# Down projection of an encoder block's FFN: ten blocks in five pairs, seven products a pair

## Chip, cores, metric

The kernel runs on one core of a Trainium2 chip. The metric is the device time of one execution in microseconds (us). The core has five engines with a queue each: PE (TensorE, matrix products into PSUM), DVE (VectorE), ACT (ScalarE), POOL (GpSimd) and SP (SyncE, which here only issues transfers). POOL issues transfers too, and only its transfers can add to what stands at their destination ("adding transfers", `accum_op=add`).

## What is computed

One layer of a hybrid encoder over 256 + 512 = 768 tokens of width 1024: three token mixers, gates, an output projection, and then the part that is changed, a SwiGLU FFN with residual:

```python
h2 = rmsnorm(x, ffn_norm_g[li])
g, up = jnp.split(h2 @ w_gate_up[li], 2, axis=-1)     # (768, 1024) @ (1024, 2 x 2816)
x = x + (jax.nn.silu(g) * up) @ w_down[li]            # (768, 2816) @ (2816, 1024)
```

All is float32.

## The kernel before

**Split numbers.** A float32 product is made of three passes: each operand is split into a high part hi (rounded to fp32r by an ACT copy) and a low part lo = x - hi (a DVE subtraction), and `mm3` (lines 756 to 758) issues hi·hi, hi·lo and lo·hi into the same PSUM tile. So every operand that PE reads costs an ACT and a DVE pass first.

**Weights.** `WStream` loads all weights in a fixed order (`W.add`), in halves of 128x1024 (512 KB, on SP's queue, three raw buffers), and `_split` makes hi and lo in rings of four tiles `wh`, `wl` each (lines 598 and 604). `W.get()` hands out the next weight and splits the one after it.

**FFN.** The 2816 hidden columns are 11 blocks of 256. For blocks 1 to 10 gate and up are products of 2x2 block matrices done with seven half-size products in place of eight (Strassen's scheme in Winograd's form): `right_factors` makes the factors of the normalized input F once, `_split_w` and `_factor` make those of each weight (five sums on POOL, lines 575 to 582; hi on ACT, line 560; lo on DVE, line 561), `block` runs the seven products of 12 matmuls of 384 columns and adds them up in two tiles `fs` (line 1412, DVE). `fin_gate` makes tanh of the gate on ACT and the gate's part of SiLU on DVE (line 1369) into `act_in` (tile `fa`); `fin_up` multiplies by up (line 1374; on POOL for blocks 1 to 10) and splits the result into the hidden activations `hid` (lines 1375, ACT, and 1376, DVE). Block 0 goes the plain way through `first`.

`down(fb)` is plain: for each of six tiles of 128 tokens and each half of the 1024 output columns, 2 x 3 matmuls of 512 columns into a PSUM tile `dn`, which DVE adds to the running output `x1` (line 1440). The order is gate 0, up 0, down 0, gate 1, up 1, and then for each further block gate `fb`, down `fb - 1`, up `fb`; the last down stores the output rows.

**PSUM.** In this stage there are eight banks: five of kind d, three of kind b. `down` takes one of each by turns, gate and up take d.

**Order of the work.** The program is written as one sequence; a planner with a timeline of its own then orders each engine's queue, by the place in the program and by what it estimates to be ready. `tc.keep_in_program_order` holds an instruction at its place. At run time every queue runs strictly in that order.

Of the kernel before, what the change touches and what calls it, by code (L numbers as in the profile page):

```python
# [504 lines left out]
class WStream:  # L505
# [2 lines left out]

    HALF = 1024

    def __init__(self, nc, tc, ctx):
# [18 lines left out]

    def _dma(self):
        i, h = divmod(self.n_dma, 2)
        ap, kk, cols, _ = self.src[i]
        t = self.praw.tile([128, self.HALF], F32, name=f"wr{i}_{h}", tag="wr")
        k2 = kk // 2
        tv = t.rearrange("p (k c) -> p k c", k=k2)
        n = cols // len(ap)
# [24 lines left out]
    def _split_w(self, i, h):  # L564
# [18 lines left out]
        self._factor(i, "S4", s4)  # L583
        self._factor(i, "A22", A22)

    def _split(self):
        i, h = divmod(self.n_split, 2)
        self.n_split += 1
        kind = self.src[i][3]
        if kind == "w":  # L590
# [7 lines left out]
        self.nc.scalar.activation(hi, r, AF.Copy)  # L598
        if self.by_dma:

            self.nc.scalar.activation(lo, r, AF.Copy, scale=-1.0)  # L601
            self.nc.gpsimd.dma_start(lo, r.bitcast(F32R), accum_op=ALU.add)  # L602
            return
        self.sub.tensor_tensor(out=lo, in0=r, in1=hi.bitcast(F32), op=ALU.subtract)  # L604
# [11 lines left out]
    def get(self, ahead=True):  # L616
        i = self.next
        self.next += 1
        if ahead:
            self.ahead(i + 1)  # L620
        _, kk, cols, kind = self.src[i]
        p = self.parts.pop(i)
        if kind == "w":
            return p
        k2 = kk // 2
        at = lambda t, k, c0, n: t[:, cols * (k % k2) + c0 : cols * (k % k2) + c0 + n]
        return lambda k, c0, n: tuple(at(t, k, c0, n) for t in p[k // k2])


def hybrid_block(ctx, tc, A, outs, consts):  # L630
# [45 lines left out]
    ones = cp.tile([128, 1], F32, name="ones")  # L676
    v.memset(ones, 1.0)
    subg = cp.tile([128, 1], F32, name="subg")


    warm = env.psa("warm")
# [41 lines left out]
    for what, fb in order:  # L723
        if what == "down":
            W.add(wd[:, 2 * fb : 2 * fb + 2, :], 2, 1024, "x")
        else:
            W.add(cols("w_gate_up", 256 * fb + (DFF if what == "up" else 0)), 8, 256, "w" if fb else None)


    def rsqrt(x, n, tag, bufs=4):  # L730

        i = sm.tile([128, n], I32, name=uid("rqi"), tag=f"rqi{n}")
        y = sm.tile([128, n], F32, name=uid("rqy"), tag=tag, bufs=bufs)
        t = sm.tile([128, n], F32, name=uid("rqt"), tag=f"rqt{n}")
# [97 lines left out]
    z_scr = [dr.tile([128, TOK], F32, name=f"z_scr{m}") for m in range(8)]  # L832
    gl_scr = [dr.tile([128, TOK], F32, name=f"gl_scr{m}") for m in range(24)]
    br_scr = [dr.tile([128, TOK], F32, name=f"br_scr{m}") for m in range(8)]
    mo_scr = [dr.tile([128, 8, TOK], F32, name=f"mo_scr{w}") for w in "hl"]


# [530 lines left out]
        act.activation(t[:, 0:n], c, AF.Tanh, scale=0.5)  # L1368
        v.scalar_tensor_tensor(out=act_in[fb][:, m, cs], in0=t[:, 0:n], scalar=1.0, in1=c, op0=add, op1=mul)

    def fin_up(fb, c, m, cs, eng=v):
        hh, hl = hid[fb]
        o = act_in[fb][:, m, cs]
        eng.tensor_tensor(out=o, in0=o, in1=c, op=mul)
        act.activation(hh[:, m, cs], o, AF.Copy, scale=0.5)
        v.scalar_tensor_tensor(out=hl[:, m, cs], in0=o, scalar=0.5, in1=hh[:, m, cs].bitcast(F32),
                               op0=mul, op1=sub)

    def new_block(what, fb):
        if what == "gate":  # L1380
            act_in[fb] = fa.tile([128, 2, TOK], F32, name=uid("fa"), tag="fa")
        else:
# [15 lines left out]
    def block(what, fb):  # L1398
# [18 lines left out]
        kw = {} if what == "gate" else {"eng": gp}  # L1417
        act.activation(c12, prod("A11", "B11"), AF.Copy)
        plus(c11, c12, prod("A12", "B21"))
        fin(fb, c11, 0, h1, **kw)  # L1420
# [5 lines left out]
        fin(fb, c22, 1, h2, **kw)  # L1426
        plus(c12, c12, prod("S4", "B22"))
        fin(fb, c12, 0, h2, **kw)
        plus(c21, c21, prod("A22", "T4"))
        fin(fb, c21, 1, h1, **kw)  # L1430

    def down(fb, last):
        w = W.get()
        x = hid.pop(fb)
        for tt in (3, 4, 5, 0, 1, 2) if fb else range(TILES):
            for c0 in (0, 512):
                ps = (psd if c0 else env.psb)("dn")
                dense_tm(ps, w, c0, 512, x, tt, 2)
                o = x1[tt][:, c0 : c0 + 512]
                v.tensor_tensor(out=o, in0=o, in1=ps, op=add)  # L1440
                if last:
                    nc.sync.dma_start(os_[tt][:, c0 : c0 + 512], o)


    with ExitStack() as c5:
# [92 lines left out]
        fa = c6.enter_context(tc.tile_pool(name="ffa", bufs=1))  # L1538
        ft_ = c6.enter_context(tc.tile_pool(name="fft", bufs=2))
        po, rs = [None] * TILES, [None] * TILES  # L1540

        def out_rows(w, c, kh, tt):
# [49 lines left out]
        rows(5)  # L1592


    W.extra = tuple(c6.enter_context(tc.tile_pool(name="wx" + w, bufs=1)) for w in "hl")
    W.sums = c6.enter_context(tc.tile_pool(name="wsum", bufs=3))
    tp = c6.enter_context(tc.tile_pool(name="ffT", bufs=1))
    fh = c6.enter_context(tc.tile_pool(name="ffh", bufs=1))
# [51 lines left out]
    down(0, False)  # L1650
    next(factors)
    next(factors, None)
    for what, fb in order[3:]:
        if what == "down":
            down(fb, fb == NFB - 1)
        else:
            block(what, fb)
    c6.close()
    x1ctx.close()

# [42 lines left out]
```

## Time and profile before

| | us |
|---|---|
| median of 3 runs | 1786.9 (1786.52 to 1790.95) |
| the profiled execution | 1785.8, of it 1784.0 span |
| PE, DVE, ACT, POOL busy | 1762.8, 1296.6, 871.6, 266.4 |
| FFN, from the first gate matmul to the end | 1266.7 to 1784.0 |
| one block of gate, down, up | about 45.5 |

A row of groups reads: line, engine, operation, output and input tiles, their shapes, count | busy time, mean ns of one | idle time of the engine just before them and what ended it. A row of waits: engine, tile and line that waited, what for: us in total, times, longest. A row of the order of time: start, duration, instruction, in brackets the idle time before it. A row of one tile or line: count: shortest, median, longest ns, first and last start. Durations of neighbours on an engine overlap a little, since an instruction starts before the one ahead has left the pipeline.

### The profile page before, as it was taken

The page shows a single profiled execution, that of the slowest core. Times are in us where ns is not written, and L with a number is a line of the kernel's source. Part 1 is how long each engine was busy: PE and PEld are TensorE (multiplying, and loading weights), DVE is VectorE, ACT ScalarE, POOL GpSimd, SP SyncE. Part 2 cuts the span into 40 slices and gives each one's busy share as a digit, 9 for nine tenths or more (in the row PEclk, how much of TensorE's full clock was granted, in tenths as well). Part 3 has the DMA queues.
Part 4 walks back from the last instruction along what each step waited for, and adds up shares of the span by engine and source line. Part 5 has one row for each costly group of instructions (what it writes and reads, how often), then busy time and mean ns, then how long its engine had stood idle before and what let it go on. Part 6 is the DMA issues. An engine that isn't in the chain of part 4 may idle for free.

```text
span 1784.0 us, 29452 instructions
## 1 busy us (share of the span) xinstructions
PE 1762.8 (99%) x11286; PEld 1625.7 (91%) x11286; DVE 1296.6 (73%) x2385; ACT 871.6 (49%) x1842; POOL 266.4 (15%) x280
## 2 busy tenths in 40 slices
PE   8999999999999999999999999999999999999998
PEld 8999988999999998999979888888889999999997
DVE  7655748799999579778875545442699777777775
ACT  7444544777676367778765433232333333333331
POOL 0000000000000101011110101000114333333330
PEclk9999999999999999999999999999999999999999
DMA  7222656655656477454862534331312222222221
GB/s 254 72 96 95 111 137 161 150 143 133 155 143 153 126 179 191 109 113 97 177 165 83 207 127 159 116 111 54 83 48 71 71 71 72 71 71 71 72 71 71
DMA packets 194797, 207.88 MB, mean 117 GB/s; under 512 B 57824, under 2 KB 167648, under 8 KB 194656
## 3 DMA queue, kind: packets, MB, share of 16 engines
q1 hardware_dynamic: 174656, 147.27, 27.9%
q0 software_dynamic: 18848, 55.58, 14.0%
q10 hardware_dynamic: 1152, 3.15, 0.5%
q8 instruction: 89, 1.46, 0.3%
q14 instruction: 52, 0.43, 0.1%
HBM read 146.11 MB, written 32.57 MB: 100 GB/s over the span
## 4 chain that ended last, share of the span: by engine, by line
PE 92%; DVE 3%; DMA 2%; ACT 1%; issue 1%; SPq 0%; POOL 0%; DVEq 0%; ACTq 0%; POOLq 0%
PE gl L756 4%; PE gl L757 4%; PE gl L758 4%; PE br L757 3%; PE br L756 3%; PE br L758 3%; PE dn L756 3%; PE dn L757 3%; PE dn L758 3%; PE gate L756 3%; PE gate L757 3%; PE gate L758 3%; PE up L756 3%; PE up L758 3%; PE up L757 3%; PE qk L756 2%
## 5 line engine op out<-in xcount | busy, mean ns | idle before, releaser
L598 ACT ACTIVATE wh<-wr 128x1024 fp32r<-128x1024 f32 x146 | 163.7, 1122 | 104.6 <-PE br L757 27.8
L604 DVE TENSOR_TENSOR wl<-wr,wh 128x1024 fp32r<-128x1024 f32 x100 | 130.7, 1307 | 92.1 <-ACT wh L598 91.3
L756 PE MATMUL gl<-Hhi,wh 128*128 128x256 f32 (+1 forms) x384 | 132.4, 345 | 1.1 <-ACT glt L1065 1.1
L1440 DVE TENSOR_TENSOR x<-x,dn 128x512 f32<-128x512 f32 x132 | 89.0, 685 | 57.5 <-PE dn L758 57.3
L758 PE MATMUL gl<-Hhi,wl 128*128 128x256 f32 (+1 forms) x384 | 129.0, 336 | 0.0
L757 PE MATMUL gl<-Hlo,wh 128*128 128x256 f32 (+1 forms) x384 | 128.9, 336 | 0.0
L602 POOL DMA_DIRECT2D wl<-wr x46 | 40.2, 873 | 518.0 <-ACT wl L601 486.3
L756 PE MATMUL qk<-wh,Hhi 128*128 128x256 f32 x384 | 108.4, 282 | 1.6 <-ACT qksq L1131 1.6
L757 PE MATMUL qk<-wl,Hhi 128*128 128x256 f32 x384 | 108.6, 283 | 0.0
L758 PE MATMUL qk<-wh,Hlo 128*128 128x256 f32 x384 | 108.5, 283 | 0.0
L560 ACT ACTIVATE wh_S<-ws 128x512 fp32r<-128x512 f32 x70 | 41.7, 623 | 130.8 <-PE dn L758 104.1
L756 PE MATMUL dn<-wh,hidh 128*128 128x512 f32 x264 | 102.5, 390 | 1.2 <-DVE x L1440 1.0
L757 PE MATMUL dn<-wl,hidh 128*128 128x512 f32 x264 | 103.0, 390 | 0.0
L758 PE MATMUL dn<-wh,hidl 128*128 128x512 f32 x264 | 100.9, 390 | 0.0
L756 PEld LDWEIGHTS gl<-Hhi,wh 128*128 128x128 f32 x384 | 72.3, 188 | 8.3 <-ACT glt L1065 1.3
L758 PEld LDWEIGHTS gl<-Hhi,wl 128*128 128x128 f32 x384 | 72.1, 188 | 8.0
L757 PEld LDWEIGHTS gl<-Hlo,wh 128*128 128x128 f32 x384 | 72.3, 188 | 7.1
L756 PEld LDWEIGHTS qk<-wh,Hhi 128*128 128x128 f32 x384 | 73.0, 190 | 2.5 <-ACT qksq L1131 1.8
L1231 DVE TENSOR_REDUCE nm<-sc 128x1 f32<-128x512 f32 (+1 forms) x96 | 57.1, 598 | 24.7 <-PE sc L1226 23.5
L758 PEld LDWEIGHTS qk<-wh,Hlo 128*128 128x128 f32 x384 | 73.1, 190 | 0.7
L757 PEld LDWEIGHTS qk<-wl,Hhi 128*128 128x128 f32 x384 | 73.1, 190 | 0.5
L1233 ACT ACTIVATE p<-sc,nm 128x512 f32<-128x512 f32 (+1 forms) x96 | 59.0, 616 | 12.4 <-DVE nm L1231 11.9
(455 smaller groups left out, 5944.9 us busy)
## 6 DMA issues: line engine op xcount, KB each, us to landing
wr<-in_w_in_dram SPq DMA_DIRECT2D x48, 512.0 KB, 5.5
wl<-wr POOLq DMA_DIRECT2D x46, 512.0 KB, 5.1
wr<-in_w_gate_up_dram SPq DMA_DIRECT2D x44, 512.0 KB, 3.5
wr<-in_w_branch_dram SPq DMA_DIRECT2D x24, 512.0 KB, 4.2
wr<-in_w_down_dram SPq DMA_DIRECT2D x22, 512.0 KB, 3.7
glr<-gl_scr POOLq DMA_DIRECT2D x24, 384.0 KB, 3.7
wr<-in_w_mem_kv_dram SPq DMA_DIRECT2D x16, 512.0 KB, 3.4
wr<-in_w_in_dram SPq DMA_DIRECT2D x32, 256.0 KB, 4.4
```

The costliest lines, as they stand in the source:

```text
L560: self.nc.scalar.activation(f(hi), src, AF.Copy)
L598: self.nc.scalar.activation(hi, r, AF.Copy)
L602: self.nc.gpsimd.dma_start(lo, r.bitcast(F32R), accum_op=ALU.add)
L604: self.sub.tensor_tensor(out=lo, in0=r, in1=hi.bitcast(F32), op=ALU.subtract)
L756: pe.matmul(ps, wh, xh, start=start, stop=False)
L757: pe.matmul(ps, wh, xl, start=False, stop=False)
L758: pe.matmul(ps, wl, xh, start=False, stop=stop)
L1231: v.tensor_reduce(out=nm[:, m : m + 1], in_=ps, axis=AX.X, op=ALU.max, negate=True)
L1233: act.activation(pm[:, 0:n], ps, AF.Exp, bias=nm[:, m : m + 1], accum_out=s1s[:, tt : tt + 1] if m == 0 else s2)
L1440: v.tensor_tensor(out=o, in0=o, in1=ps, op=add)
```

## The change

Blocks 1 to 10 are taken in pairs (1,2), (3,4), ... (9,10). The down projection of a pair is a 2x2 block product: A11, A21 are the two token halves of the first block's activations, A12, A22 those of the second; B11, B12 are the column halves of the first block's `w_down` rows, B21, B22 those of the second's. Seven products of half size (384 tokens x 256 x 512 columns, three PSUM tiles each) take the place of eight. The order becomes gate, up, gate, up, down of the pair.

The sums of the weights (T1 to T4) are made by adding transfers from DRAM (`_split_d`), those of the activations by DVE (`left_sum`); `left` and `_right` split them. Products that belong to one output quarter are added to `x1` by DVE at once (`into`). The three that belong to several quarters (P1, P6, P5) are copied out by ACT and added up over the pairs in DRAM tiles `p_scr` by adding transfers (`keep`); `down_sums` loads them in the last pair, between gate 9 and up 9, and DVE adds them to the quarters. Quarter (1,0) takes quarter (1,1) along, which is why (1,1) is subtracted from it once at block 2. The last pair does not go through `p_scr`: it adds P1 and P1 + P6 to `x1` by adding transfers in SBUF.

`hid` and its splits remain for block 0 only; `fin_up`'s multiplication goes from POOL to DVE; the ring of extra tiles for down weights goes; `act_in` has two buffers, the `ft` tiles (tanh, and now the copies of products) three.

```diff
 # WStream
+    def _right(self, i, key, src):
+        hi, lo = self._tile(f"{i}_{key}")
+        self.nc.scalar.activation(hi, src, AF.Copy)
+        self.nc.vector.tensor_tensor(out=lo, in0=src, in1=hi.bitcast(F32), op=ALU.subtract)
...
+    def _split_d(self, i, h, kind):
...
+        add = lambda t, b: self.nc.gpsimd.dma_start(t.rearrange("p (k c) -> p k c", k=2), b, accum_op=ALU.add)
+        minus = lambda t, x: self.nc.scalar.activation(t, x, AF.Copy, scale=-1.0)
+        new = lambda k: self.wsums.tile([128, self.HALF], F32, name=f"wt{i}{k}", tag="wt")
+        if kind == "d" and h == 0:
+            self._right(i, "B11", r)
+            self.z = new("z")
+            minus(self.z, r)
+            add(self.z, b12)
+        elif kind == "d":
+            self.x = new("x")
+            minus(self.x, r)
+            add(self.x, b22)
+            self._right(i, "T3", self.x)
+        elif h == 0:
+            add(self.x, b11)
+            self._right(i, "T2", self.x)
+            self._right(i, "T1", self.z)
+            self._right(i, "B21", r)
+        else:
+            minus(self.x, self.x)
+            add(self.x, b21)
+            self._right(i, "T4", self.x)
+            self._right(i, "B22", r)
 # order of the weights
-    order = [("gate", 0), ("up", 0), ("down", 0), ("gate", 1), ("up", 1)]
-    for fb in range(2, NFB):
-        order += [("gate", fb), ("down", fb - 1), ("up", fb)]
-    order.append(("down", NFB - 1))
...
+        elif fb % 2 == 0:
+            for b, kind in ((fb - 1, "d"), (fb, "e")):
+                W.add([wd[:, 2 * b : 2 * b + 2, 512 * c : 512 * c + 512] for c in range(2)], 4, 512, kind)
 # fin_up
-        eng.tensor_tensor(out=o, in0=o, in1=c, op=mul)
-        act.activation(hh[:, m, cs], o, AF.Copy, scale=0.5)
...
+        v.tensor_tensor(out=o, in0=o, in1=c, op=mul)
+        if fb == 0:
...
 # block
+        if what == "up" and fb % 2 == 0:
+            W.ahead(W.next + 1)
...
-    def down(fb, last):
...
+    def left(key, src):
+        hi, lo = (lf.tile([128, 2, HT], F32R, name=uid(f"l{key}{w}"), tag="l" + w) for w in "hl")
+        act.activation(hi, src, AF.Copy, scale=0.5)
+        v.scalar_tensor_tensor(out=lo, in0=src, scalar=0.5, in1=hi.bitcast(F32), op0=mul, op1=sub)
+        L[key] = hi, lo
...
+    def down_begin(fb):
+        a = act_in[fb]
+        left("A11", a[:, :, 0:HT])
+        left("S3", left_sum(None, a[:, :, 0:HT], a[:, :, HT:TOK], sub))
...
+    def into(r, c, y, op=add, done=False, pin=False):
+        for t in range(3):
+            o = out_block(r, c, t)
+            i = v.tensor_tensor(out=o, in0=o, in1=y[t], op=op)
...
+            if done:
+                nc.sync.dma_start(os_[3 * r + t][:, 512 * c : 512 * c + 512], o)
+    def down_pair(fb, last):
...
+        def prod(l, r):
+            (lh, ll), (rh, rl) = L.pop(l), R.pop(r)
+            ps = [(psd if t else env.psb)("dn") for t in range(3)]
+            for t in range(3):
+                sl = slice(128 * t, 128 * t + 128)
+                for k in range(2):
+                    mm3(ps[t], lh[:, k, sl], ll[:, k, sl], rh[:, k], rl[:, k], k == 0, k == 1)
+            return ps
...
+        def keep(key, ps):
+            e = copies(ps)
+            for t in range(3):
+                gp.dma_start(p_scr[key][t], e[t], **({"accum_op": add} if fb > 1 else {}))
+        p1 = prod("A11", "B11")
+        s1 = left_sum(None, a21, a22, add)
+        s2 = left_sum(None, s1, a11, sub)
+        left("S2", s2)
+        if last:
+            e = copies(p1)
+            for t in range(3):
+                gp.dma_start(out_block(0, 0, t), e[t], accum_op=add)
+        else:
+            keep("1", p1)
+        p7 = prod("S3", "T3")
+        left("S1", s1)
+        into(1, 1, p7, pin=last)
+        if last:
+            into(1, 0, p7)
+        p6 = prod("S2", "T2")
+        left("A12", a12)
+        if last:
+            for t in range(3):
+                v.tensor_tensor(out=e[t], in0=e[t], in1=p6[t], op=add)
+            for r, c in ((1, 1), (1, 0), (0, 1)):
+                for t in range(3):
+                    gp.dma_start(out_block(r, c, t), e[t], accum_op=add)
+        else:
+            keep("6", p6)
+        p5 = prod("S1", "T1")
+        left("A22", a22)
+        left("S4", left_sum(s2, a12, s2, sub))
+        if last:
+            into(0, 1, p5)
+            into(1, 1, p5, done=True)
+        else:
+            keep("5", p5)
+        into(0, 0, prod("A12", "B21"), done=last)
+        into(1, 0, prod("A22", "T4"), done=last)
+        into(0, 1, prod("S4", "B22"), done=last)
+    def down_sums():
+        for t in range(3):
+            e = {}
+            for key in "165":
+                e[key] = ft_.tile([128, 512], F32, name=uid("de"), tag="ft")
+                nc.sync.dma_start(e[key], p_scr[key][t])
...
+            plus(b[0, 0], e["1"])
+            plus(e["6"], e["1"])
+            plus(b[1, 1], e["6"])
+            plus(b[1, 0], b[1, 1])
+            plus(b[1, 1], e["5"])
+            plus(e["6"], e["5"])
+            plus(b[0, 1], e["6"])
 # the loop
-    for what, fb in order[3:]:
...
+    for fb in range(1, NFB):
+        block("gate", fb)
+        if fb == NFB - 2:
+            down_sums()
+        if fb == 2:
+            into(1, 0, [out_block(1, 1, t) for t in range(3)], sub)
+        if fb % 2 == 0:
+            down_begin(fb - 1)
+        block("up", fb)
+        if fb % 2 == 0:
+            down_pair(fb - 1, fb == NFB - 1)
```

More of the change, by code (lines that the diff above doesn't have):

```diff
@@ L834, in hybrid_block @@
     br_scr = [dr.tile([128, TOK], F32, name=f"br_scr{m}") for m in range(8)]
+    p_scr = {k: [dr.tile([128, 512], F32, name=f"p_scr{k}{t}") for t in range(3)] for k in "165"}
     mo_scr = [dr.tile([128, 8, TOK], F32, name=f"mo_scr{w}") for w in "hl"]
@@ L1440, in down, with left_sum @@
                 v.tensor_tensor(out=o, in0=o, in1=ps, op=add)
-                if last:
-                    nc.sync.dma_start(os_[tt][:, c0 : c0 + 512], o)
+    L = {}
+    def left(key, src):
[3 more added lines that the diff above has]
+        L[key] = hi, lo
+    def left_sum(o, x, y, op):
+        if o is None:
+            o = stg.tile([128, 2, HT], F32, name=uid("ls"), tag="brr")
+        v.tensor_tensor(out=o, in0=x, in1=y, op=op)
+        return o
@@ new lines, in down_pair, with copies @@
+    def down_pair(fb, last):
+        a, b = act_in.pop(fb), act_in.pop(fb + 1)
+        a11, a21, a12, a22 = a[:, :, 0:HT], a[:, :, HT:TOK], b[:, :, 0:HT], b[:, :, HT:TOK]
+        R = dict(W.get())
+        R.update(W.get())
+        def prod(l, r):
[6 more added lines that the diff above has]
+            return ps
+        def copies(ps):
+            e = [ft_.tile([128, 512], F32, name=uid("de"), tag="ft") for t in range(3)]
+            for t in range(3):
+                act.activation(e[t], ps[t], AF.Copy)
+            return e
+        def keep(key, ps):
[38 more added lines that the diff above has]
+        into(0, 1, prod("S4", "B22"), done=last)
@@ new lines, in down_sums @@
+    def down_sums():
+        for t in range(3):
+            e = {}
+            for key in "165":
+                e[key] = ft_.tile([128, 512], F32, name=uid("de"), tag="ft")
+                nc.sync.dma_start(e[key], p_scr[key][t])
+            b = {(r, c): out_block(r, c, t) for r in range(2) for c in range(2)}
+            plus = lambda o, y: v.tensor_tensor(out=o, in0=o, in1=y, op=add)
+            plus(b[0, 0], e["1"])
[5 more added lines that the diff above has]
+            plus(b[0, 1], e["6"])
@@ L1649, in hybrid_block @@
                     next(factors)
-    down(0, False)
+    down_first()
     next(factors)
     next(factors, None)
-    for what, fb in order[3:]:
[L1654 to L1657, printed above, removed]
+    fhctx.close()
+    lf = c6.enter_context(tc.tile_pool(name="ffl", bufs=3))
+    W.wsums = c6.enter_context(tc.tile_pool(name="wsum2", bufs=2))
+    for fb in range(1, NFB):
[9 more added lines that the diff above has]
+            down_pair(fb - 1, fb == NFB - 1)
     c6.close()
```

63 lines of the change are left out of this document (39 added, 24 removed).

## The prediction

> **What bounds the kernel now.** I read the page's busy shares and chain first, then the busy time by stretches, then PE's own order of time in one block, then the groups and waits of the stretch in which the changed work lies.
>
> ```profile
> PE 1762.8 (99%) x11286; PEld 1625.7 (91%) x11286; DVE 1296.6 (73%) x2385; ACT 871.6 (49%) x1842; POOL 266.4 (15%) x280
> PE 92%; DVE 3%; DMA 2%; ACT 1%; issue 1%; SPq 0%; POOL 0%; DVEq 0%; ACTq 0%; POOLq 0%
> ```
>
> TensorE is busy nearly all the time and carries 92% of the chain that ended last. An average can hide a stage with another limit, so the FFN is read by itself:
>
> ```profile
> core 0: us, PE busy (x) PEld busy (x) DVE busy (x) ACT busy (x) POOL busy (x), PEclk, DMA share, GB/s
> 1284.00:1368.00 84.00, 81.83 (x417) 74.26 (x416) 73.93 (x92) 32.05 (x51) 30.20 (x19) 1.00 0.20 63
> ...
> 1413.00:1459.00 46.00, 46.00 (x245) 43.12 (x244) 36.26 (x52) 15.37 (x27) 17.39 (x12) 1.00 0.22 69
> 1459.00:1505.00 46.00, 46.00 (x244) 43.06 (x243) 36.36 (x52) 14.98 (x26) 17.74 (x13) 1.00 0.22 69
> ...
> 1733.00:1784.00 51.00, 46.47 (x224) 40.35 (x222) 28.47 (x42) 6.17 (x10) 5.04 (x5) 1.00 0.17 62
> ```
>
> The two middle rows are one block each (gate, down, up): PE has no idle time, at full clock, and DVE is second with 36.3 of 46 us. Who waits says the same:
>
> ```profile
> PE dn L756 <- DVE x L1440: 1.0, 1, 1.0
> PE up L756 <- ACT fs L1418: 1.0, 1, 1.0
> ...
> DVE x L1440 <- PE dn L758: 51.0, 79, 0.7
> ```
>
> From 1190 us to the end PE waits for others about 3 us in all (both 1 us waits are before 1350, where DVE makes the factors of F), while DVE waits 51 us for the down projection between 1368 and 1760. So a matmul taken out of the FFN is time, as long as DVE, second in line, can follow.
>
> **The change, part by part.** *Matmuls removed.* Before, a down block is 6 row tiles x 2 column halves x 2 k x 3 = 72 matmuls, 144 for a pair. After, a pair is 7 products x 3 tiles x 2 k x 3 = 126. Five pairs drop 90 matmuls of the same shape (128x128 by 128x512). The 390 ns that the groups give for one overlaps its neighbours; what counts is the distance in PE's order of time:
>
> ```profile
> 1368.15 0.40 PE L758 MATMUL dn<-wh,hidl 128*128 128x512 f32 x1
> ...
> 1383.82 0.39 PE L758 MATMUL dn<-wh,hidl 128*128 128x512 f32 x1
> ...
> 1388.23 0.34 PE L756 MATMUL up<-T2h,wh_A 128*128 128x384 f32 x1
> ...
> 1392.39 0.34 PE L756 MATMUL up<-T3h,wh_S 128*128 128x384 f32 x1
> ```
>
> There are 69 steps between the first two rows, 0.227 us each; 24 between the last two, 0.173 us. So the saving is 90 x 0.227 = 20.4 us. A pair of blocks on PE was 336 x 0.173 + 144 x 0.227 = 90.9 us and becomes 58.2 + 28.6 = 86.8. The Trainium skill, TensorE: Matmul & The Clock Gate, section Back-to-back issue gap, gives about 131 ns for a sustained stream of 512-column matmuls; by that the saving would be 11.8 us. The trace's 227 ns for these fp32r ones decides.
>
> *DVE.* Its load has to fit into the shorter 86.8 us. The groups between 1368 and 1760:
>
> ```profile
> L1440 DVE TENSOR_TENSOR x<-x,dn 128x512 f32<-128x512 f32 x108 | 73.2, 686 | 51.1 <-PE dn L758 51.0
> L561 DVE TENSOR_TENSOR wl_S<-ws,wh_S 128x512 fp32r<-128x512 f32 x59 | 48.0, 837 | 0.3
> L561 DVE TENSOR_TENSOR wl_A<-wr,wh_A 128x512 fp32r<-128x512 f32 x40 | 39.7, 1023 | 8.4 <-ACT wh_A L560 8.4
> L1369 DVE SCALAR_TENSOR_TENSOR fa<-ft,fs 128x384 f32<-128x384 f32 x34 | 37.6, 1105 | 1.5
> L604 DVE TENSOR_TENSOR wl<-wr,wh 128x1024 fp32r<-128x1024 f32 x18 | 22.1, 1226 | 18.0 <-ACT wh L598 17.8
> L1376 DVE SCALAR_TENSOR_TENSOR hidl<-fa,hidh 128x384 fp32r<-128x384 f32 x33 | 17.5, 548 | 0.0
> ```
>
> and the size that the new left factors and sums have (128x768), from the factors of F:
>
> ```profile
> L1630 DVE TENSOR_TENSOR fB<-fB,fB x2: 956/957/958, 1306.2 to 1307.7; 128x768 f32<-128x768 f32 x2
> L749 ACT ACTIVATE T3h<-fB x2: 848/848/849, 1307.2 to 1308.7; 128x768 fp32r<-128x768 f32 x2
> ```
>
> A pair has 72 us of DVE work before (two blocks, scaled to 90.9 us). Out go 12 of 24 adds of dn (8.2), 4 splits of 1024-wide weights (4.9) and 8 of hidl (4.4); in come 7 splits in `_right` (8.6), 7 of `left` and 4 `left_sum` at 0.957 (10.5) and the 8 multiplications of `fin_up`, which were POOL's, at 0.56 (4.5). Sum 78.1.
>
> On top stands what POOL does to DVE:
>
> ```profile
> L1440 DVE TENSOR_TENSOR x<-x,dn x132: 673/687/689, 1313.0 to 1779.7; 128x512 f32<-128x512 f32 x132
> L1369 DVE SCALAR_TENSOR_TENSOR fa<-ft,fs x40: 548/560/1653, 1337.1 to 1735.3; 128x384 f32<-128x384 f32 x40
> L561 DVE TENSOR_TENSOR wl_S<-ws,wh_S x70: 680/687/1775, 1305.6 to 1750.0; 128x512 fp32r<-128x512 f32 x70
> ...
> L1374 POOL TENSOR_TENSOR fa<-fa,fs 128x384 f32<-128x384 f32 x34 | 39.8, 1180 | 56.3 <-DVE fs L1412 56.3
> ```
>
> Adds with one input in PSUM never stretch (689 ns at most); operations with both inputs in SBUF do, by up to 1.09 us. Over their medians the three groups wl_S, wl_A and L1369 lose 59 x 0.150 + 40 x 0.336 + 34 x 0.545 = 40.8 us in 8.6 blocks, 9.5 us a pair, to 24 POOL instructions: 0.40 us each. L1374 takes 8 of the 24 with it, so 3.2 us come back: low end 75. High end: every one of the 16 left (`_split_w`) now meets a DVE operation with two SBUF inputs, of which there are more, and costs the full 1.09: 17.4 in place of 9.5, 86. I take 77, near the rows. This stretching is what the Trainium skill, SBUF — State Buffer, section Who interferes with whom, calls an exclusive lock: a DVE instruction with two SBUF inputs against a GpSimd one that reads SBUF, the loser waiting the whole instruction. The trace agrees (560 against 1653 ns), and the rule speaks against the change, which trades immune adds for exposed ones.
>
> So DVE goes from 72 of 90.9 to some 77 of 86.8. It also idles 9.7 us a block now, 5.9 of it for dn; the other 3.8 (7.6 a pair) are waits in its queue, as for wh at L604. 77 + 7.6 = 84.6 still fits. But the load is uneven: the down stretch of 28.6 us gets 12 adds, 5 lefts, 3 sums, 7 factors of the next gate and up to 5 `_right` splits, 8.2 + 7.7 + 6.4 + 6.1 = 28.4. Cover: the five d banks of PSUM, some 8 us of PE work. I charge 0.5 us to each of the first four pairs: 2 (0 to 28, the upper end below).
>
> *The last pair.* `down_sums` stands between gate 9 and up 9: 21 adds of 512 columns with both inputs in SBUF, at 0.687 14.4 us, less some overlap of neighbours: 13.5. Its nine loads on SP's queue need the three `ft` buffers that gate's tanh also uses, and the weight loads of blocks 9 and 10 stand behind them. The last `down_pair` makes 24 DVE adds for 12 (+8.2), and there is no next gate to split (-6.4). DVE gets 77 + 15.3 = 92.3 against 86.8: 5.5 us late (3 to 14 with the ends above).
>
> *ACT and the adding transfers.* ACT loses 8 hidh and 4 splits and gains 7 lefts at 0.85, 7 splits and 3 negations at 1.06 and 9 evacuations at about 0.63 (512 columns, between the rows of 384 and 768):
>
> ```profile
> L598 ACT ACTIVATE wh<-wr 128x1024 fp32r<-128x1024 f32 x18 | 19.1, 1061 | 32.4 <-DMA wr<-in_w_down_dram 17.9 <-PE dn L758 12.4 <-ACT fs L1418 1.4
> L1375 ACT ACTIVATE hidh<-fa 128x384 fp32r<-128x384 f32 x33 | 17.2, 522 | 25.7 <-POOL fa L1374 25.7
> L602 POOL DMA_DIRECT2D wl<-wr x46: 853/860/1003, 297.3 to 1269.5; - x46
> DMA to landing us min/median/max: 4.5/5.1/7.6
> ```
>
> That is 30 - 8.4 + 22 = 44 of 86.8 us, no bound. POOL loses 8 x 1.18 and gains 13 issues x 0.86, about even. An add into DRAM is in no trace; the nearest is the 512 KB add into SBUF, 5.1 us to land. `keep` has three `ft` buffers: P6's copies (8.2 us after P1's) find them free if 3 x 0.86 + landing stays under some 7 us; P5's copies come 4.1 us after P6's and wait some 4 us, with the next gate's ACT splits behind them. Cover: P5 holds three banks, PE has P2 and most of P4 (about 7 us) in the other five. Cost 0 at 5.1 us, taken; from about 8 us on a stall, rival below. Nothing here can give a gain.
>
> *Start.* `down_first` has no extra tile for its weights and takes them from the ring of four, so its second 1024-wide split (1.2 us) falls into the DVE-bound stretch up to 1349; block 1's four multiplications come to DVE (2.2) and its four hidl go (2.2). Plus 1 (0 to 3). The smaller rsqrt rings are written and read on DVE in order: nothing.
>
> *Tail.* Now:
>
> ```profile
> 1779.72 0.69 DVE L1440 TENSOR_TENSOR x<-x,dn 128x512 f32<-128x512 f32 x1 [0.44 <-PE dn L758]
> out_dram<-x SPq DMA_DIRECT2D x12, 256.0 KB, 2.0
> ```
>
> After, it is again one add of 512 and a store. The nine adding transfers into x1 after P6 need 9 x 0.86 + 5 = 13 us, P5 to P3 take 16.4: hidden, though DVE's adds of P5 wait for them in its queue; counted in the 5.5.
>
> Sum: -20.4 + 2 + 5.5 + 1 = -11.9. The profiled execution took 1785.8 (span 1784.0 and 1.8 around it), so 1773.9; the median of the runs shown, 1786.9, is 1.1 above it: 1775.
>
> **The rivals.** *Clean:* DVE at its low end and `down_sums` spread by the planner: 1786.9 - 20.4 + 1 = 1767. For it: PE has not one wait in ten blocks today. Against: the last pair's 92 us of DVE.
>
> *DVE becomes the bound (slower).* Mechanism: POOL's 16 sums a pair block DVE's two-SBUF operations, and DVE's queue waits stay. Place: from gate 2 on. At the high end DVE needs 86 + 7.6 = 93.6 a pair, 6.8 over PE: 5 x 6.8 = 34, and 15.3 in the last: 1786.9 - 20.4 + 34 + 15.3 + 1 = 1817. It decides from about 4 us of PE idle per pair, that is when DVE, waits included, needs 91. For it: half the DVE operations are exposed already and stretch by up to 1.09 us. Against: DVE's own work fits with 10 us to spare at 77, and waits shrink when it is behind.
>
> *Adding into DRAM is slow.* If it lands in 10 us, P6's copies wait 5 for P1's, and P5's wait for P6's until some 4 us of PE idle are left in each of four pairs: 1775 + 16 = 1791, no change. For it: no row shows it. Against: half the bytes of the 5.1 us row.
>
> **How the numbers follow.** Forecast 0.62 (its own range 1768 to 1781), clean 0.13, slow transfers 0.10, DVE bound 0.15. What a measurement tells from no change is about 0.3%, 5.4 us. Faster 0.75, same 0.10, slower 0.15. The range 1765 to 1788 takes in the first two and part of the third.
>
> **What would show it.** 702 dn matmuls at the same 0.227 us; a steady pair of 87 to 88 us with PE idle under 1 us; DVE near 77 in it; PE waits for DVE between gate 9 and the end, some 5 us; the multiplications at L1374's place on DVE between 0.55 and 1.6. Wrong if PE idles over 2 us in the pairs before the last, whichever of DVE's adds, a left factor or an evacuation it waits for.

## The result, and the profile after

| | before | after |
|---|---|---|
| median, us | 1786.9 (4 runs) | 1810.5 (4 runs, 1807.8 to 1812.1) |
| ratio | 1 | 1.0125, 95% interval 1.0105 to 1.0146 |
| profiled execution, its span | 1785.8, 1784.0 | 1811.9, 1810.1 |

The changed kernel is 1.25% slower, where 0.7% faster was forecast: 1810 lies outside the range of 1765 to 1788. The page of the changed kernel shows these busy shares and this chain of work that ended last:

```profile
PE 1757.0 (97%) x11196; PEld 1615.4 (89%) x11196; DVE 1315.8 (73%) x2431; ACT 929.1 (51%) x1906; POOL 281.2 (16%) x308
DMA 3%; issue 1%; DVE 1%; PE 1%; POOL 1%; ACT 0%; DVEq 0%; SPq 0%; POOLq 0%; ACTq 0%
```

The 90 matmuls are gone (11286 to 11196), and PE's share fell from 99 to 97%: PE has less to do, and it waits longer than what it saved. The chain is no help here: its shares add up to 7% of the span. So I read the time by stretches that begin at a pair's first gate matmul. The first row runs from the first gate matmul to gate 2, the others are pairs 2 to 4 and the last pair; pair 1 is left out. The columns are those of the view before the change (PE, PEld, DVE, ACT and POOL busy, granted clock, DMA share, GB/s):

```profile
1270.20:1362.80 92.60, 85.60 (x466) 76.50 (x465) 80.26 (x110) 33.73 (x55) 29.47 (x17) 0.98 0.23 63
...
1422.00:1514.40 92.40, 89.07 (x463) 82.81 (x462) 70.95 (x106) 42.26 (x67) 36.47 (x29) 0.98 0.51 117
1514.40:1607.20 92.80, 89.06 (x463) 82.95 (x462) 70.07 (x103) 41.83 (x66) 35.98 (x29) 0.98 0.51 116
1607.20:1699.60 92.40, 88.90 (x464) 82.85 (x463) 69.58 (x103) 41.90 (x66) 36.51 (x29) 0.98 0.52 117
1699.60:1799.40 99.80, 91.86 (x463) 84.11 (x461) 85.90 (x128) 35.55 (x54) 35.97 (x28) 0.97 0.52 124
```

A pair was to take 86.8 us of PE time. Pairs 2 to 4 take 92.4 to 92.8, the last 99.8, and the granted clock is below 1. DVE has 70 of 92 us in pairs 2 to 4, so it is not the bound. The waits of PE from 1270 us on (engine, tile, line waited for whom: us in total, times, longest) name what is:

```profile
PE dn L798 <- ACT lS4h L1493: 10.4, 4, 3.5
PE up L798 <- ACT fs L1461: 3.9, 1, 3.9
PE dn L798 <- ACT lS2h L1493: 3.3, 1, 3.3
...
PE gate L799 <- DVE flo L792: 2.3, 1, 2.3
```

**Where the time went**, from the spans (1810.1 - 1784.0 = 26.1 us):

| stretch | measured against | after | us |
|---|---|---|---|
| up to the first gate matmul | before: 1266.7 | 1270.2 | +3.5 |
| start: first gate to gate 2 | before: 86.4 | 92.6 | +6.2 |
| 90 matmuls fewer, 0.227 each | | | -20.4 |
| pair 1, from gate 2 to gate 3 | steps alone: 57.8 | 59.2 | +1.4 |
| pairs 2 to 4 | 87.0 each | 277.6 | +16.6 |
| last pair | 87.0 | 99.8 | +12.8 |
| last matmul's end to the end of the span | before: 4.3 | 10.7 | +6.4 |

They add up to 26.5, against 26.1; the small rest fits the idle time that the kernel before had in the same blocks. The first row lies ahead of the changed work and moves between 1265 and 1272 in the profiles of these kernels, so it isn't put down to the change. A pair of about 87 us is called clean from here on.

**The stall of pairs 2 to 4.** PE's order of time at the end of pair 2:

```profile
1503.18 0.39 PE L800 MATMUL dn<-wh_T,lA22l 128*128 128x512 f32 x1
1506.64 0.50 PE L798 MATMUL dn<-wh_B,lS4h 128*128 128x512 f32 x1 [3.07 <-ACT lS4h L1493]
...
1508.20 0.64 PE L798 MATMUL dn<-wh_T,lA22h 128*128 128x512 f32 x1
...
1511.62 0.46 PE L798 MATMUL dn<-wh_B,lS4h 128*128 128x512 f32 x1
1511.92 0.40 PE L799 MATMUL dn<-wl_B,lS4h 128*128 128x512 f32 x1
...
1514.20 0.39 PE L800 MATMUL dn<-wh_B,lS4l 128*128 128x512 f32 x1
```

Two costs show here. PE waits 3.07 us for the high part of S4. Then, from 1508.20 to 1511.62, eight steps take 3.42 us, 0.427 each, and from 1511.92 the ten steps to 1514.20 take 0.228 again. The granted clock (the last but two of the columns) in that stretch:

```profile
1509.50:1513.00 3.50, 3.50 (x12) 2.80 (x11) 3.50 (x7) 1.70 (x4) 2.12 (x2) 0.68 0.89 181
```

Eight steps at 0.2 more are 1.6 us on top of a 3 us gap. ACT's queue shows why S4 is late:

```profile
1492.61 0.60 ACT L1543 ACTIVATE de<-dn 128x512 f32<-128x512 f32 x1 [0.81 <-DMA p_scr<-de]
...
1496.40 0.59 ACT L1543 ACTIVATE de<-dn 128x512 f32<-128x512 f32 x1
1505.26 0.60 ACT L1543 ACTIVATE de<-dn 128x512 f32<-128x512 f32 x1 [8.27 <-DMA p_scr<-de]
1505.75 0.83 ACT L1493 ACTIVATE lS4h<-ls 128x768 fp32r<-128x768 f32 x1
```

P6's three copies are made by 1497. The first copy of P5 needs one of their `ft` buffers, waits 8.27 us for P6's adding transfers, and S4's split stands right behind it. The POOL queue in the same time:

```profile
1485.31 3.17 POOL L1549 DMA_DIRECT2D p_scr<-de  x3
1496.59 2.31 POOL L578 TENSOR_TENSOR ws<-wr,wr 128x512 f32<-128x512 f32 x1 [8.12 <-DMA wr<-in_w_gate_up_dram]
1498.99 1.28 POOL L579 TENSOR_TENSOR ws<-ws,wr 128x512 f32<-128x512 f32 x1
1500.24 1.28 POOL L583 TENSOR_TENSOR ws<-wr 128x512 f32<-128x512 f32 x1
1501.47 2.63 POOL L1549 DMA_DIRECT2D p_scr<-de  x3
```

Between P1's and P6's transfers stand three weight sums of the next gate, and the first of them waits until 1496.59 for its load. P6's transfers, whose data lay ready from 1492.6 to 1497, are issued from 1501.47 on.

### The profile page after: what moved, and what is told of

Read it like the earlier page. It is cut to its first block, busy times and chain, and to the rows that moved or that the text cites. A ratio compares the mean times of both kernels' runs of the same rounds, so it can differ in the third digit from the quotient of the medians.

```text
span 1810.1 us, 29578 instructions
## 1 busy us (share of the span) xinstructions
PE 1757.0 (97%) x11196; PEld 1615.4 (89%) x11196; DVE 1315.8 (73%) x2431; ACT 929.1 (51%) x1906; POOL 281.2 (16%) x308
## 5 line engine op out<-in xcount | busy, mean ns | idle before, releaser
L638 ACT ACTIVATE wh<-wr 128x1024 fp32r<-128x1024 f32 x126 | 142.9, 1134 | 72.8 <-PE br L799 27.9
L644 DVE TENSOR_TENSOR wl<-wr,wh 128x1024 fp32r<-128x1024 f32 x80 | 106.5, 1332 | 74.3 <-ACT wh L638 73.2
L564 DVE TENSOR_TENSOR wl_S<-ws,wh_S 128x512 fp32r<-128x512 f32 x70 | 55.1, 812 | 9.8 <-ACT wh_S L563 9.6
L1627 ACT ACTIVATE glr<-glr 128x768 f32<-128x768 f32 x24 | 20.3, 846 | 65.6 <-DMA glr<-gl_scr 64.1
L798 PE MATMUL v<-wh,Hhi 128*128 128x256 f32 x192 | 53.9, 281 | 0.0
L799 PE MATMUL v<-wl,Hhi 128*128 128x256 f32 x192 | 53.8, 280 | 0.0
```

The lines of the kernel that those rows point to most:

```text
L564: self.nc.vector.tensor_tensor(out=f(lo), in0=src, in1=f(hi).bitcast(F32), op=ALU.subtract)
L798: pe.matmul(ps, wh, xh, start=start, stop=False)
L799: pe.matmul(ps, wh, xl, start=False, stop=False)
L1627: act.activation(g, g, AF.Tanh, scale=0.5)
```

## The experiments

The comparisons are with the kernel before on the same chip (medians 1786.2 to 1787.7). Stretches and waits come from one profiled execution of each kernel.

| kernel | median, us | ratio to before, 95% interval |
|---|---|---|
| e1_plain | 1797.3 | 1.0050 (1.0033 to 1.0066) |
| e2_pool_order | 1792.5 | 1.0025 (1.0016 to 1.0034) |
| e3_p5_direct | 1787.2 | 0.9996 (0.9987 to 1.0005) |
| e4_before_ring2 | 1790.5 | 1.0013 (1.0004 to 1.0022) |
| e5_start | 1784.8 | 0.9989 (0.9979 to 0.9999) |
| e6_tail | 1783.6 | 0.9982 (0.9972 to 0.9991) |
| e7_sums | 1794.0 | 1.0036 (1.0022 to 1.0051) |
| e8_all | 1790.5 | 1.0016 (1.0007 to 1.0026) |
| e9_all_pinned | 1781.2 | 0.9964 (0.9953 to 0.9976) |
| e10_pool_tail | 1779.6 | 0.9963 (0.9950 to 0.9976) |
| e11_extra | 1785.4 | 0.9992 (0.9982 to 1.0001) |
| e12_spread | 1782.1 | 0.9971 (0.9961 to 0.9982) |

Theory A: adding into DRAM is slow. Theory B: POOL's order makes P6's transfers late. Theory C (the rival on record): DVE is the bound. The first three kernels tell them apart.

**e1_plain**: the changed kernel with plain transfers in place of adding ones; it leaves out the summing over the pairs.

```diff
-                gp.dma_start(p_scr[key][t], e[t], **({"accum_op": add} if fb > 1 else {}))
+                gp.dma_start(p_scr[key][t], e[t], **{})
```

> Leaves out the summing over pairs: every pair overwrites the DRAM tiles instead of adding to them; nothing else changes. In the changed kernel pairs two to four take 92.4 to 92.8 us from gate to gate, 5.5 more than their matmuls (87.0), and TensorE waits there 3.1 to 3.5 us a pair for the high part of S4 on ScalarE, which stands behind a copy of P5 that waits up to 8.3 us for an `ft` buffer. Theory A (adding into DRAM is itself slow): the waits go, pairs of 87 to 88 us, the kernel about 15 us faster (1795). Theory B (the adds are late because they stand behind the next gate's weight sums in POOL's queue): pairs stay within 1.5 us of 92.5, like the first pair's own wait of 7.1 us that occurs with plain writes; 1808 to 1812.

The pairs 2 to 4 took 88.3, 88.8 and 88.8 us and the waits for S4 0.5 to 1.0. The transfers of this kernel (line, count: shortest, median, longest ns of issue; then landing):

```profile
L1549 POOL DMA_DIRECT2D p_scr<-de x36: 540/542/1089, 1393.1 to 1680.1; - x36
...
DMA to landing us min/median/max: 2.3/4.7/6.8
```

and of the changed kernel:

```profile
L1549 POOL DMA_DIRECT2D p_scr<-de x36: 540/878/1742, 1396.8 to 1694.7; - x36
...
DMA to landing us min/median/max: 2.3/6.0/9.3
```

Adding costs 0.34 us more to issue and 1.3 us more to land, in the medians. The landing stays well under the 10 us of the rival on record, yet without the adding some 4 of the 5.5 us a pair are gone: the wait itself is 2 to 2.5 us shorter, and these gaps of under 1 us are not followed by half-clock steps. A is a part of the cause.

**e2_pool_order**: the adding transfers stay; the next gate's weight sums are queued behind P6's.

```diff
-        R.update(W.get())
+        R.update(W.get(False))
+        W.ahead(W.next, 0)
...
-            keep("6", p6)
+            with tc.issue_after(keep("6", p6).ins):
+                W.ahead(W.next)
```

> The next gate's weight sums (five on POOL) are queued behind the three adding transfers of P6 instead of ahead of them; its raw loads are issued as before. Theory B: P6's adds are issued right behind their copies, the copies of P5 wait at most 3 us, TensorE no longer waits for S4; pairs two to four fall from 92.5 to 87 to 89 us, the kernel to 1795 to 1800. Theory A: P5's copies still wait 6 us or more for landings, pairs above 91, 1805 to 1811.

Pairs 2 and 3 by stretches (pair 4 takes 86.9 us), and ACT's wait for the transfers from 1413 to 1690 us:

```profile
1420.40:1507.30 86.90, 86.90 (x463) 81.81 (x462) 68.08 (x98) 41.26 (x65) 32.33 (x28) 1.00 0.54 120
1507.30:1594.50 87.20, 87.16 (x464) 81.86 (x463) 73.25 (x104) 41.67 (x66) 35.33 (x30) 1.00 0.54 126
```

```profile
ACT de L1544 <- DMA p_scr<-de: 14.0, 14, 2.1
```

The pairs are clean, with adding transfers that land in 5.8 us in the median: ACT's longest wait for them falls from 8.8 to 2.1 us and hides. So mending B takes the whole stall away, and A alone makes none: the transfers have to be late and slow, both, to cost 5.5 us. The median is 2.5 us below the lower end of what was expected.

**e3_p5_direct**: P5 is not copied and kept but added by DVE to its three quarters in every pair.

```diff
-            keep("5", p5)
+            into(1, 1, p5)
+            into(1, 0, p5, sub)
+            into(0, 1, p5)
...
```

> P5 is no longer copied and added up in DRAM: VectorE adds it from PSUM to quarters (1,1) and (0,1) and subtracts it from (1,0), which later takes (1,1) along; nine adds of 0.69 us (6.2 us a pair) for three copies, three adding transfers and, in the last pair, three loads and six adds. If the stall is the ScalarE queue standing behind P5's copies (A and B both), pairs two to four fall to 87 to 89 us and the kernel to 1792 to 1800. If VectorE's load is what costs (the rival of the prediction), 6 more us of it make the pairs longer than 92.5 and the kernel slower than 1811.

Pair 4 and the last pair:

```profile
1591.20:1678.50 87.30, 87.13 (x464) 81.81 (x463) 75.29 (x110) 40.25 (x63) 32.49 (x26) 1.00 0.49 116
1678.50:1773.00 94.50, 88.97 (x463) 81.29 (x461) 85.54 (x126) 35.51 (x55) 35.37 (x29) 1.00 0.52 118
```

Pairs 2 to 4 take 86.9, 87.1 and 87.3 us, clean again, though POOL's order is as in the changed kernel: no copy of P5 means no wait ahead of S4. DVE takes nine more adds a pair (75 to 76 of 87 us) and PE does not notice, so C is refuted for the pairs before the last. With fewer sums from DRAM the last pair falls from 99.8 to 94.5, which may be why the median lies 4.8 us below the range that was expected. The kernel now equals the one before: the start, the last pair and the tail still eat the 20.4 us. All that follow but e4 build on it.

**e4_before_ring2**: the kernel before with the smaller rsqrt rings alone.

```diff
-        i = sm.tile([128, n], I32, name=uid("rqi"), tag=f"rqi{n}")
+        few = 2 if n == TILES * 4 else 4
+        i = sm.tile([128, n], I32, name=uid("rqi"), tag=f"rqi{n}", bufs=few)
...
```

> The kernel before with only the change's smaller rings (two buffers instead of four) for the temporaries of the 24-column reciprocal square root in the query-key stage. The changed kernel's first score matmul starts at 671.6 us against 669.1. If the rings cost it: this kernel is 2 to 3.5 us slower than before (1789 to 1790.5). If that shift comes from another order of the whole program: within 1 us of 1786.9.

It is 0.13% slower (0.04 to 0.22%), so the rings may cost something. In its profile the first score matmul starts at 672.6 us, where the kernel before is at 669.1; but e1 and e3, which have the same rings, reach it as early as the kernel before (668.8 and 669.2). The mechanism stays open.

**e5_start**: e3 with an extra tile for down 0's weights (as before the change) and with the three subtractions of quarter (1,1) held behind up 2 (the two activation buffers lie in pools of their own, to make room). **e11_extra**: the extra tile alone.

```diff
-            W.add(wd[:, 0:2, :], 2, 1024)
+            W.add(wd[:, 0:2, :], 2, 1024, "x")
...
+        if fb == 2:
+            into(1, 0, [out_block(1, 1, t) for t in range(3)], sub, pin=True)
...
```

> On top of the kernel with P5 added directly (1787.2): down 0 gets its extra weight tile back, and the three subtractions of quarter (1,1) from (1,0) are held at their place behind up 2 instead of floating into the stretch where VectorE makes the factors of F. From the first gate to gate 2 the kernel before takes 86.4 us, the changed one 92.6, the one with P5 direct 92.6. If these two edits are the loss at the start: 86 to 88 us for this stretch, kernel 1781 to 1784. If the load of gate 1's weights or something else holds it: stretch above 91, 1786 to 1788.

> P5 direct and only the extra tile for down 0's weights; the subtractions float as in the changed kernel. From the first gate to gate 2 P5 direct takes 92.6 us, with both start edits 85.9. If the weight ring is the larger part (it also delayed the load and the POOL sums of gate 1's weights by 26 us): 87 to 89. If the three floating subtractions (0.68 to 1.77 us each on VectorE there) are the larger part: 90 to 92.

In the changed kernel the start shows two things: POOL's first sums for gate 1, and the subtractions on DVE.

```profile
1308.90 3.25 POOL L578 TENSOR_TENSOR ws<-wr,wr 128x512 f32<-128x512 f32 x1 [36.02 <-DMA wr<-in_w_gate_up_dram]
...
1335.14 0.68 DVE L1516 TENSOR_TENSOR x<-x 128x512 f32<-128x512 f32 x1
...
1339.85 1.77 DVE L1516 TENSOR_TENSOR x<-x 128x512 f32<-128x512 f32 x1
1341.54 1.75 DVE L792 TENSOR_TENSOR flo<-fB,fhi 128x1536 fp32r<-128x1536 f32 x1
```

In the kernel before the sums began at 1282.85. The subtractions belong to block 2, but the planner put them just ahead of `flo`, for which PE then waited 2.26 us. From the first gate to gate 2 in e11, then the same in e5 with pair 1 behind it (the changed kernel took 92.6 and 59.2):

```profile
1267.50:1359.20 91.70, 85.59 (x465) 77.00 (x464) 77.39 (x110) 33.39 (x54) 25.91 (x17) 0.98 0.23 64
```

```profile
1265.10:1351.00 85.90, 83.44 (x466) 75.50 (x465) 74.67 (x103) 33.42 (x55) 24.36 (x16) 1.00 0.24 68
1351.00:1414.50 63.50, 60.79 (x295) 54.70 (x294) 52.92 (x80) 28.68 (x42) 16.81 (x17) 0.95 0.48 125
```

In this stretch the extra tile alone gives 0.9 us; with the subtractions moved as well, it is 6.7. But what the moving gave was lost again at once: pair 1 takes 63.5 us where e11 and e3 take 57.7. PE waits 2.71 us for S2 there, and half-clock steps follow. Held behind up 2, the three subtractions (1.89 us) stand ahead of S2's sum on DVE, which had also waited 4.03 us for a weight split (2.36 in e11). From the first gate to gate 3 both e5 and e11 take 149.4 us, and e3 takes 150.3.

**e6_tail**: e3, and in the last pair DVE adds P1 and P1 + P6 to `x1`, not adding transfers.

```diff
-            for t in range(3):
-                gp.dma_start(out_block(0, 0, t), e[t], accum_op=add)
+            into(0, 0, p1)
...
-                    gp.dma_start(out_block(r, c, t), e[t], accum_op=add)
+                into(r, c, e)
...
```

> On top of P5 direct: in the last pair P1 and P1 + P6 are added to the output by VectorE (12 more adds of 0.68 us) instead of 12 adding transfers on POOL. With the transfers, 12.7 us pass from the last matmul to the end (4.1 in the kernel before). If VectorE's adds of the later products stand behind the landings: 4 to 7 us from the last matmul to the end, kernel 1779 to 1783. If VectorE's load is the bound at the end, its 8 us more make it no faster: 1786 to 1790.

The end of the changed kernel:

```profile
1785.50 7.97 POOL L1574 DMA_DIRECT2D x<-de  x9 [11.68 <-DVE de L1571]
...
1799.00 0.39 PE L800 MATMUL dn<-wh_B,lS4l 128*128 128x512 f32 x1
...
1802.12 0.69 DVE L1516 TENSOR_TENSOR x<-x,dn 128x512 f32<-128x512 f32 x1 [2.35 <-DMA x<-de]
1804.23 1.88 DVE L1516 TENSOR_TENSOR x<-x,dn 128x512 f32<-128x512 f32 x3 [1.42 <-DMA x<-de]
```

and of e6:

```profile
1769.56 8.45 DVE L1516 TENSOR_TENSOR x<-x,dn 128x512 f32<-128x512 f32 x14
```

From the last matmul to the end e3 had 12.7 us and e6 has 6.7; the last adds run without a break. Some of the gain is lost again, as the last pair takes 96.5 us, 1.9 more. In the medians 3.6 us are left.

**e7_sums** and **e8_all**: `down_sums` in tiles of their own and in two parts, t = 0 behind gate 9 and t = 1, 2 behind up 9, not held in place; e8 adds the edits of e5 and e6.

```diff
-                e[key] = ft_.tile([128, 512], F32, name=uid("de"), tag="ft")
+                e[key] = tile2[:, 512 * j : 512 * j + 512]
...
-            down_sums()
+            down_sums((0,))
...
```

> On top of P5 direct: the sums loaded back from DRAM use the two tiles of the weight sums instead of the three `ft` tiles, and two of the three row tiles come behind up 9 instead of behind gate 9. From gate 9's first to the last matmul P5 direct takes 94.5 us, its matmuls 87. If the ring of `ft` (tanh behind the loads) and the burst of adds are the loss: 88 to 91 us, kernel 1781 to 1785. If VectorE's sum of work in the last pair is the loss (92 against 87 by the prediction): above 93, 1786 to 1788.

> The three edits on top of P5 direct together. If the three losses are separate they add up: start -5, last pair -4, tail -7, kernel 1770 to 1775 with the matmuls' own gain of 20.4 us nearly whole. If VectorE bounds the end as a whole, the last pair and the tail give one gain, not two: 1776 to 1780.

Both miss. PE's waits in e7:

```profile
PE up L798 <- DVE fs L1456: 6.4, 3, 4.1
PE gate L798 <- DVE x L1516: 3.1, 1, 3.1
```

Freed from the `ft` ring, the sums were drawn forward by the planner, ahead of gate 9's work on DVE. At 1680.32 the first of them waits 3.22 us for its load with DVE's adds of the pair's last products behind it, and PE then waits for DVE at 1684.9 and 1705.8 us. It is the mishap of the start once more: adds with nothing due float into a stretch that has no room for them.

**e9_all_pinned** and **e10_pool_tail**: the extra tile, the subtractions held behind gate 2, the sums held in place (t = 0 behind gate 9, t = 1, 2 behind gate 10) and DVE's tail; in e10 POOL adds P1 + P6 to two of its three quarters.

```diff
+            plus = lambda o, y: tc.keep_in_program_order(v.tensor_tensor(out=o, in0=o, in1=y, op=add))
...
+        elif fb == NFB - 1:
+            down_sums((1, 2))
...
+                    gp.tensor_tensor(out=o, in0=o, in1=e[t], op=add)
...
```

> P5 direct, the extra tile for down 0, VectorE's adds at the end, and the sums from DRAM and the three subtractions held at their place in VectorE's queue: the first row tile's sums behind gate 9, the other two behind gate 10, the subtractions behind gate 2. In the run with the sums moved but free, the planner had put them ahead of gate 9 and TensorE waited 3.1 and 4.1 us there for VectorE; if those waits were VectorE standing behind sums whose loads had not landed, they go, the last pair takes 88 to 90 us to its last matmul, and the kernel comes to 1773 to 1778. If VectorE's total at the end is the bound, the last pair plus tail stays at the 102 us of the run with the tail edit alone and the kernel at 1779 to 1783 (the start's gain only).

> As the one before, but six of the last pair's adds (P1 + P6 into quarters (0,1) and (1,0)) are done by POOL instead of VectorE. If VectorE's backlog of adds makes the end (about 7 us from the last matmul to the end where the kernel before needs 4.1): 2 to 4 us faster than the one before. If POOL's adds hold VectorE's (both read two SBUF operands) or come too late for P5's and P4's adds: same within 1 us or slower.

e10 by stretches (pair 1, pairs 2 to 4, the last pair):

```profile
1352.50:1414.10 61.60, 59.61 (x296) 53.82 (x295) 53.79 (x80) 28.75 (x42) 17.34 (x17) 0.97 0.49 129
1414.10:1674.70 260.60, 260.60 (x1388) 245.76 (x1387) 225.32 (x335) 121.17 (x189) 98.67 (x79) 1.00 0.49 116
1674.70:1771.70 97.00, 90.48 (x463) 82.13 (x461) 90.59 (x132) 35.80 (x55) 33.62 (x23) 0.98 0.36 95
```

Pairs 2 to 4 take 260.6 us, 86.9 each, with PE never idle; the start is as short as before the change (85.9 against 86.4), and the tail is 6.1 us. Both kernels beat the one before and the changed one; e10 is 0.37% (0.24 to 0.50) below the former and some 30 us below the latter. What e10 has over e9 is within their spread. Of the 20.4 us some 6 are left: pair 1 takes 3.8 us more than its steps, the last pair is 10 us over clean, and the tail 1.8 over the kernel before. In pair 1 PE waits 1.99 us for S2; the subtractions now stand ahead of a weight split that comes before S2 in its queue, and how much of the wait they make is not shown. The last pair's largest waits are new ones, 5.3 us for the splits of T3 and T2.

Held in place, the sums no longer cost what they cost in e8: last pair and tail together take 102.4 us in e9, where e8 took 113.1. But e6, with the sums still in the `ft` ring, took 103.2, so moving them into tiles of their own gained next to nothing there. That is the second of e9's two alternatives, in which DVE's total work at the end is the bound; DVE is busy for 90.3 of the last pair's 96.6 us in e9. Whether that load or the late splits of T3 and T2 sets the time of the last pair is not shown.

**e12_spread**: e10 with one third of the sums each behind gate 9, up 9 and gate 10, so that the tiles of the weights' sums come free sooner.

```diff
         elif fb == NFB - 1:
-            down_sums((1, 2))
+            down_sums((2,))
...
+        if fb == NFB - 2:
+            down_sums((1,))
```

> The previous version, with the sums of the second of the three token tiles moved from behind gate 10 to behind up 9 (one third of the sums each behind gate 9, up 9 and gate 10). Theory: in the previous version PE still waits 5.3 us in the last down projection for T3 and T2, because the two tiles of the weights' sums are held by the sums from DRAM until these are added behind gate 10 (ACT waited 4.2 and 3.3 us for those adds). If so, the first wait is gone or under 1 us, the second shrinks too, and with the half-clock steps behind the waits 3 to 6 us go: 1774 to 1777. Rival: T3 and T2 are late because the adding transfers of the weights' sums and ACT's copies follow each other one by one (about 9 us each); then the waits stay at 4 to 5 us and the time at 1779 to 1780.

The waits of PE and of ACT from 1715 to 1770 us:

```profile
PE dn L798 <- ACT wh_T L592: 4.7, 2, 2.4
...
ACT wt91x L601 <- DVE x L1601: 4.2, 1, 4.2
```

The theory's number failed: the waits stay at the rival's 4 to 5 us, the last pair takes 100.6 us, and 1782.1 is not below e10. But it decides less than it was meant to, since the tile of T3 is still held for 4.2 us, now by the adds of the third token tile alone. Whether that tile or the chain of transfer, split and next transfer through it makes T3 and T2 late stays open.

## Why the prediction was wrong, point by point

**The saving was right.** 90 matmuls at 0.227: the steps in the changed kernel are 0.228, and clean pairs (e2, e3, e10) take 86.9 to 87.3 us, against the 86.8 forecast and the 0.5 charged for DVE's uneven load.

**DVE was right as no bound of the steady pairs, and costed too high**: 70 to 71 us a pair in the changed kernel and 68 to 73 in e2, where 77 was taken and 75 was the low end. The rival that DVE becomes the bound fell with e3, for the pairs before the last.

**The step that failed is "ACT and the adding transfers ... Cost 0".** It saw that P5's copies would wait, some 4 us, and it named the next gate's splits as the work behind them. The wait was 8.27 us, and the work behind them was the split of S4, which PE needs in the same down projection. And it took P6's transfers as issued when their copies were ready. POOL was costed as a sum of busy times ("about even"), not as a queue: each of its weight sums that waits for a load holds back all that follows. What was charged at 0 cost 16.6 us in three pairs. The rival "adding into DRAM is slow" had the right place, from a wrong condition: the landing was 6.0 us, not 10, and e2 is clean with it. That its 16 us are near the 16.6 is luck: it had 4 us of idle PE in each of four pairs, where there were 5.5 in three, a good quarter of that from the clock, and 1.4 in pair 1.

**The granted clock was in no step.** The prediction counted a wait as its length; each of the three waits for S4 was followed by seven or eight half-clock steps, which cost 1.5 to 1.6 us, a good quarter of the 5.5 us a pair.

**The last pair was mis-sized**: 5.5 against 12.8. The working had DVE's extra load (DVE is busy for 85.9 of the 99.8 us); it did not follow the sums' loads through the `ft` ring. The changed kernel's ACT and PE:

```profile
1752.86 0.52 ACT L1411 ACTIVATE ft<-fs 128x384 f32<-128x384 f32 x1 [4.27 <-DVE de L1597]
...
1761.03 0.69 PE L798 MATMUL up<-fhi,wh_S 128*128 128x384 f32 x1 [3.85 <-ACT fs L1461]
```

Tanh waits for a tile that the sums hold, and PE behind it. The prediction had named that ring, and gave it no price. A second wait of PE, 3.27 us at 1777.08, is for S2, whose split stands in ACT's queue behind a weight split that waits 2.56 us for an adding transfer of the weights' sums. With the half-clock steps behind them the two waits make some 10.8 of the 12.8 us. This is read from the trace alone: the runs without the ring (e7 to e10) got other waits in its place, so what it costs by itself is not shown.

**The tail was called hidden**, since nine transfers need 13 us and the products from P5 to P3 take 16.4. They were issued from 1785.50 on, 13.9 us before PE's end, as POOL had waited 11.68 us for DVE's P1 + P6, and DVE's adds stand in order behind each of them: 6.4 us. With DVE's adds in their place e6 ends 6.0 us sooner after its last matmul than e3, and its last pair gives up 1.9.

**The start was mis-sized**: 1 (0 to 3) against 6.2. The ring of four was seen; that the subtractions would be planned into the full stretch was not, and e11 against e5 shows that moving them is worth 5.8 of the 6.7 us in this stretch; pair 1 then loses as much.

**The rsqrt rings** were put at nothing: e4 is 0.04 to 0.22% slower, and why is open.

## What to carry to other kernels

Cost every engine that issues transfers as a queue in order, not as a sum: ask what each transfer stands behind, who waits for its landing, and what stands behind that waiter. When the bound engine has no idle time, the extra work of a scheme that saves it 1% is worth as much as the saving; work without a due time (loose adds, sums kept for later) has to be given a place, or it lands where there is no room; and the place has to have room: what e5 gained at the start by moving the subtractions it lost in pair 1. And let the last pass of a loop be costed by itself, for there the cover of the next pass is missing.

## What the runs showed of the hardware

After PE gaps of 2 us and more the steps were often about half as fast, mostly for 3 to 3.5 us. The stretch in the changed kernel above is one, and this is one of the two shortest gaps in the FFN that did it (e10; in e12 it was 1.97 us):

```profile
1391.93 0.50 PE L798 MATMUL dn<-wh_T,lS2h 128*128 128x512 f32 x1 [1.99 <-ACT lS2h L1493]
...
1392.81 0.63 PE L799 MATMUL dn<-wl_T,lS2h 128*128 128x512 f32 x1
...
1395.80 0.51 PE L800 MATMUL dn<-wh_T,lS2l 128*128 128x512 f32 x1
```

Seven steps in 2.99 us are 0.427 each. In e5 it lasted 6.1 us (1391.15 to 1397.27), at a granted clock of 0.51. It does not follow every gap: after 3.28 us in e2 (1758.4) the steps stayed at 0.23. Gaps of 1.7 us or less in the FFN were not followed by it, but for one of 0.95 us in e12 (1750.63), 2.6 us behind one of 2.29 us; and in an earlier stage of the kernel before a gap of 1.85 us was (675.33), 4 us behind one of 1.62 us. The Trainium skill, TensorE: Matmul & The Clock Gate, section Part 1: The HAM clock gate, has the array's clock halved after an idle window of some 3.4 us that runs freely, not from the kernel's own start, and whole again after a busy one. The trace agrees on the half rate (0.427 against 0.228 us a step) and on the chance in it, as gaps of one length were followed by it or not; it differs on the length of the gap, as 1.99 us were enough here.

The transfers of 256 KB into DRAM from POOL took 0.88 us to issue and 6.0 to land in the median of the changed kernel, where nine of the 36 are plain, and 0.54 and 4.7 where all are plain (e1).
